# Attention steps taken from a written list of names instead of a rule over estimated times

## The chip, the cores and the metric

The kernel runs on one core of a Trainium2 chip. The metric is the device time in microseconds (us) of the whole launch. The kernel before took 1698.75 us, the median of 3 runs (1696.91 to 1700.2).

The engines are named as in the profile: PE is the matmul engine (PEld its weight loads), DVE the vector engine, ACT the scalar engine, POOL the GpSimd engine, SP the engine that issues most of the DMAs. Each works through its own instructions strictly in the order in which the program gives them, and waits at an instruction until what it needs has been finished elsewhere.

## The reference, cut to what matters

One inference step of a two-layer encoder, in float32, on 512 prompt rows and 64 sample rows (576 columns in the kernel, which works on transposed activations). Each layer:

```python
h = rmsnorm(x, w['g_mix_norm'])
proj = h @ w['w_in']                                   # one projection for three mixers
qa, ka, va, qg, kg, vg, ag, rg, cq, ckv, kr_raw = jnp.split(proj, offsets, axis=-1)
o_a = stick_breaking_attention(qa, [past, ka], [past, va])      # "sb", 4 heads of 64
o_b = gla_recurrence(qg, kg, vg, log_a, s0) , times silu(rg)    # "gla", blocks of 16 rows
o_c = mla_attention(cq, ckv, kr_raw, ...)                       # "mla", 8 heads, latent keys
x = x + jnp.concatenate([norm(o_a), norm(o_b), norm(o_c)], -1) @ w['w_out']
x = x + memory_cross_attention(rmsnorm(x, ...), mem_k, mem_v, w)  # mem_k, mem_v from mem_prompt
h = rmsnorm(x, w['g_ffn_norm'])
x = x + (jax.nn.silu(h @ w['w_gate']) * (h @ w['w_up'])) @ w['w_down']
```

Stick-breaking attention takes scores, a running sum along the keys (a scan in the kernel) and an exponential; the mla queries are projected from a low-rank `cq`, normalised per head and rotated.

## The kernel before, in words

Large matrix products are made from float32 split in a high and a low part (`wH`, `wL` of a weight, `hH`, `hL` of an activation), three matmuls for one. Weights arrive by DMA as `wraw`; ACT makes `wH` from it and DVE makes `wL`.

The attention stage of a layer (the part that the change touches) is cut into generators. Each `yield` ends one *step*: the instructions that are issued between two yields. Several generators are alive at once, and class `Order` (from line 750) takes one step of one of them at a time. Whatever it takes is issued at once, so the order of the steps is the order in which the instructions stand on PE and, within small limits of the scheduler behind it, on DVE, ACT and POOL too.

The generators that the change and the prediction speak of, with the names of the tiles in the trace (the digit is the layer) and the letters by which the new list calls their steps:

- `win()` (line 1028, letter W): the projection, some 39 steps, most of them 24 matmuls into `win0.D`. It has rank 10, that is, it is meant as filler. Its last steps make the columns `rg` (for the gate of gla) and `cq` (for the mla queries); a `cq` step (`nat`, line 925) also issues small statistics (`win0.s`, `win0.j`) on ACT, DVE and POOL. T10 to T14 turn a tile of `cq` (`win0.T<-ident,win0.j`, results to `win0.cT`).
- sb units (`sb_units`, line 1135; b0 to b7, two alive at a time), three steps each: scores (`sb0.S<-win0.sbk,win0.qo`), which also issue the chain of copies on ACT, scans on DVE and masks on POOL that make the weights `sb0.sg`; transposes (`sb0.T<-ident,sb0.sg`) with the copies to `sb0.PT`, one on ACT and one on DVE; and the product with the values (`sb0.T<-sb0.PT,win0.sbv`). c is the norm of their output.
- the turning of the memory rows (j, `wout0.T<-ident,wout0.mem`, results to `wout0.mH` and `wout0.mL`) and the projection of the memory keys and values (k0, 8 steps of 24 matmuls into `wout0.D`).
- mla query units (`mlaq_units`, line 1197; d0 to d9, three alive): scores of one row tile (`mlaq0.S<-mlaq0.wH,win0.cT`), followed by a chain that goes back and forth between ACT, DVE and POOL, and, in a second step, transposes (`mlaq0.T<-ident,mlaq0.j`). e are the units for keys and values (`mlak0`), f the attention itself, g the norms, h the sample rows.
- the output projection `wout` (line 1251): k1 is its part for gla (16 steps of six matmuls, `wout0.D<-gla0.mix,wout0.wH`), k2 for sb, k3 for mla. Each step ends in one DVE addition `X<-X,wout0.D`. Rank 10, so filler too.

What sets the order before is the rule in `Order.run` (line 791). Class `Clock` (line 39) keeps an estimate of when each tile is written and when each engine is free. Among the live generators the rule looks at those whose inputs, by that estimate, are there by the time PE is through with what it has (plus `SLACK`), and takes the lowest rank first:

```python
now = max(clock.pe + SLACK, min(at(x) for x in free))
x = min((x for x in free if at(x) <= now), key=lambda x: (x["rank"], at(x), x["n"]))
```

The same class orders the cross attention behind it in each layer; that and the feed-forward part are not touched. Nearly every instruction is recorded at one helper line, L195, so the rows below are told apart by their tiles.

Of the kernel before, what the change touches and what calls it, by code (L numbers as in the profile page):

```python
# [216 lines left out]
def tile_hybrid(ctx, tc, ins, outs):  # L217
    clock = tc.clock = Clock()
# [528 lines left out]
    class Order:  # L747
# [23 lines left out]
        def line(self, units, depth=2, rank=0, name=None, tag="S"):  # L771

            self.lines.append({"units": list(units), "depth": depth, "rank": rank, "live": 0, "name": name, "ph": phase[0],
                               "tag": tag})
# [1039 lines left out]
```

## Time and profile before

| quantity | value |
|---|---|
| median of 3 runs | 1698.75 us (1696.91 to 1700.2) |
| the profiled execution's own time | 1699.62 us |
| its span, first to last instruction | 1697.9 us |
| PE busy | 1648.0 us (97%), 12279 instructions |
| DVE busy | 1211.8 us (71%) |
| ACT busy | 898.4 us (53%) |
| POOL busy | 206.6 us (12%) |
| chain that ended last | PE 77%, DVE 12%, ACT 4%, issue 3% |

Span less PE busy is the time in which PE did nothing, about 50 us. The launch lies 1.7 us around the span. The attention stage of layer 0 runs from about 25 to 385 us, that of layer 1 some 835 us later; between them stand cross attention and the feed-forward part, where PE has next to no idle time.

### The profile page before, as it was taken

To read this page: it belongs to the slowest core of one execution; us is meant where nothing else is said; L and a number is where in the kernel's file an instruction comes from. 1 tells how busy PE (TensorE), PEld (TensorE's weight loads), DVE (VectorE), ACT (ScalarE), POOL (GpSimd) and SP (SyncE) were. 2 spreads that over 40 slices of the span, in tenths; PEclk is the share of its full clock that TensorE was granted. 3 is DMA by queue.
4 is the path that set the end of the run, shared out by engine and by line. 5 is a ranking of instruction groups with operands and counts; after the bars stand their busy time and mean duration, and the time that the engine had idled before them with its cause. 6 is when DMAs were issued, how large, how long until landed. Compare 5 with 4: busy or idle time off the path is not lost.

```text
span 1697.9 us, 30894 instructions
## 1 busy us (share of the span) xinstructions
PE 1648.0 (97%) x12279; PEld 1534.6 (90%) x12279; DVE 1211.8 (71%) x2462; ACT 898.4 (53%) x1915; POOL 206.6 (12%) x303
## 2 busy tenths in 40 slices
...
GB/s 166 114 49 82 44 128 35 26 58 82 61 57 94 100 81 95 97 81 98 79 79 91 78 51 88 94 26 26 85 65 51 86 92 97 87 88 100 85 91 56
DMA packets 113648, 133.31 MB, mean 79 GB/s; under 512 B 10610, under 2 KB 95712, under 8 KB 113504
## 3 DMA queue, kind: packets, MB, share of 16 engines
...
q0 software_dynamic: 352, 0.03, 0.0%
...
## 4 chain that ended last, share of the span: by engine, by line
PE 77%; DVE 12%; ACT 4%; issue 3%; POOL 2%; DMA 1%; POOLq 0%; ACTq 0%; DVEq 0%; SPq 0%
PE ffn0.D L195 9%; PE ffn1.D L195 9%; PE ffn0.T L195 7%; PE ffn0.S L195 7%; PE ffn1.T L195 7%; PE ffn1.S L195 6%; PE win1.D L195 5%; PE win0.D L195 4%; PE cross0.D L195 3%; PE wout1.D L195 2%; PE wout0.D L195 2%; PE cross1.D L195 2%; PE cross1.T L195 1%; PE cross0.T L195 1%; PE mlap0.T L195 1%
## 5 line engine op out<-in xcount | busy, mean ns | idle before, releaser
L195 ACT ACTIVATE ffn1.wH<-ffn1.wraw 128x1024 fp32r<-128x1024 f32 x64 | 59.3, 927 | 116.5 <-PE ffn1.T L195 61.5
L195 ACT ACTIVATE ffn0.wH<-ffn0.wraw 128x1024 fp32r<-128x1024 f32 x64 | 59.3, 927 | 111.9 <-PE ffn0.T L195 60.8
L195 DVE TENSOR_TENSOR ffn1.sL<-ffn1.sum,ffn1.sH 128x1024 fp32r<-128x1024 f32 x40 | 48.9, 1222 | 39.7 <-ACT ffn1.sH L195 39.6
L195 DVE TENSOR_TENSOR ffn0.sL<-ffn0.sum,ffn0.sH 128x1024 fp32r<-128x1024 f32 x40 | 48.9, 1222 | 39.7 <-ACT ffn0.sH L195 39.6
L195 DVE TENSOR_TENSOR ffn0.wL<-ffn0.wraw,ffn0.wH 128x1024 fp32r<-128x1024 f32 x64 | 67.5, 1055 | 8.2 <-ACT ffn0.wH L195 7.6
L195 DVE TENSOR_TENSOR ffn1.wL<-ffn1.wraw,ffn1.wH 128x1024 fp32r<-128x1024 f32 x64 | 67.5, 1055 | 8.2 <-ACT ffn1.wH L195 7.6
L195 POOL TENSOR_TENSOR ffn0.u<-ffn0.u,ffn0.u 128x576 f32<-128x576 f32 x6 | 10.0, 1672 | 459.8 <-DVE ffn0.wL L195 452.8
L195 PE MATMUL ffn1.D<-ffn1.bT,ffn1.sH 128*128 128x288 f32 x320 | 65.1, 295 | 0.2 <-ACT ffn1.part L195 0.2
L195 PE MATMUL ffn0.D<-ffn0.bT,ffn0.sH 128*128 128x288 f32 x320 | 65.2, 295 | 0.1
L195 ACT ACTIVATE ffn0.sH<-ffn0.sum 128x1024 fp32r<-128x1024 f32 x40 | 42.2, 1056 | 21.1 <-PE ffn0.S L195 20.9
L195 ACT ACTIVATE ffn1.sH<-ffn1.sum 128x1024 fp32r<-128x1024 f32 x40 | 42.2, 1055 | 21.1 <-PE ffn1.S L195 20.9
L195 PEld LDWEIGHTS ffn1.D<-ffn1.bT,ffn1.sH 128*128 128x128 f32 x320 | 51.6, 189 | 1.0 <-ACT ffn1.part L195 0.9
L195 PEld LDWEIGHTS ffn0.D<-ffn0.bT,ffn0.sH 128*128 128x128 f32 x320 | 51.6, 189 | 0.6 <-ACT ffn0.part L195 0.3
L195 PE MATMUL ffn1.D<-ffn1.bT,ffn1.sL 128*128 128x288 f32 x160 | 47.5, 297 | 0.0
L195 PE MATMUL ffn0.D<-ffn0.bT,ffn0.sL 128*128 128x288 f32 x160 | 47.5, 297 | 0.0
L195 PE MATMUL win1.D<-win1.wH,ffn0.hH 128*128 128x256 f32 (+1 forms) x160 | 47.2, 295 | 0.0
L195 PE MATMUL win0.D<-win0.wH,in.hH 128*128 128x256 f32 (+1 forms) x160 | 46.9, 293 | 0.0
L195 PE MATMUL win0.D<-win0.wL,in.hH 128*128 128x256 f32 (+1 forms) x160 | 45.9, 287 | 0.3 <-DVE win0.wL L195 0.3
L195 PE MATMUL win1.D<-win1.wL,ffn0.hH 128*128 128x256 f32 (+1 forms) x160 | 45.8, 286 | 0.4 <-DVE win1.wL L195 0.4
L195 PE MATMUL win1.D<-win1.wH,ffn0.hL 128*128 128x256 f32 (+1 forms) x160 | 45.7, 286 | 0.0
L195 PE MATMUL win0.D<-win0.wH,in.hL 128*128 128x256 f32 (+1 forms) x160 | 45.7, 286 | 0.0
L195 ACT ACTIVATE ffn1.part<-ffn1.D 128x288 f32<-128x288 f32 x60 | 24.5, 409 | 38.8 <-PE ffn1.D L195 38.8
...
## 6 DMA issues: line engine op xcount, KB each, us to landing
...
```

What stands on the lines that cost most here:

```text
L195: r = fn(*args, **kw)
```

## The change

The rule gives way to a list, `STEPS`, of 317 step names for one layer. A generator gets a letter (and a count for each new one of its kind), and `Order.run` takes the live generator that the list names next. Only the attention stage passes a list; layer 1 uses the same one without `G0` (the gains, which only layer 0 loads). The cross attention goes on by the rule. The steps themselves, and with them every instruction, are the same; helper line L195 becomes L209.

```diff
+STEPS = """
...
+W0*3 b0 j0 W0*2 b1 b0 j0 W0*3 b0 b2 W0 b1 j0 W0 b1 W0 b3 b2 j0 T10 W0 b2 b4 b3 T11 T12 b3 b5 W0 b4 W0 b4 b6 T13 k0 b5
+k0 b5 b7 Y0 p0 b6 k0 T14 b6 Y1 p1 b7 k0 b7 Y2 c0*2 d0 d1 k0 c1 Y3 k0 d2 c1 k0 d0 d3 d1 d4 d2 d5 k0*2 k1 d3 d6 k1 d4 d7
...
+"""
@@ class Order
-        def add(self, gen, rank=0, ready=0.0, line=None, done=None, tag="T"):
+            self.count, self.taken = {}, []
+
+        def add(self, gen, rank=0, ready=0.0, line=None, done=None, tag="T", name="x"):
             self.n += 1
+            k = self.count[name] = self.count.get(name, -1) + 1
...
-        def run(self):
+        def run(self, steps=None):
+
+            steps = [w.split("*")[0] for w in (steps or "").split() for _ in range(int((w + "*1").split("*")[1]))]
             self.start()
             while self.tasks:
-                at = lambda x: max(x["ready"], clock.room(x["tag"]))
                 free = [x for x in self.tasks if x["after"] is None or x["after"] in self.events]
-                now = max(clock.pe + SLACK, min(at(x) for x in free))
-                x = min((x for x in free if at(x) <= now), key=lambda x: (x["rank"], at(x), x["n"]))
+                if steps:
+                    x = next(x for x in free if x["name"] == steps[len(self.taken)])
+                else:
+                    at = lambda x: max(x["ready"], clock.room(x["tag"]))
+                    now = max(clock.pe + SLACK, min(at(x) for x in free))
+                    x = min((x for x in free if at(x) <= now), key=lambda x: (x["rank"], at(x), x["n"]))
+                self.taken.append(x["name"])
...
-        od.run()
+        od.run(STEPS.replace("G0", "") if l else STEPS)
```

Written in the same letters, the rule's own order in the stretch of the sb units was `W0*3 b0 j0 W0 b1 b0 j0 W0*2 b0 b2 b1 j0 W0*2 b1 b3 b2 j0 T10 W0 b2 b4 b3 T11 W0*2 b3 b5 b4 T12 W0*2 b4 b6 T13 b5 k0 T14 k0 b5 b7 p0 b6 Y0 k0 b6 Y1 p1 b7 k0 b7 Y2 k0 c0*2 d0 d1 c1`, and then `Y3 k0 d2 c1 k0 d0 d3 d1 d4 d2 d5 k0*2 k1 d3 d6 d4 d7 d5 d8 k1*3 d6 d9 e0 k1 d7 k1*2 d8 k1 d9 e1 e2`. From `d3 d6` on the new list has, behind one k1, `d4 d7 k1*2 d5 d8 k1*2 d6 d9 e0 k1 d7 k1*2 d8 k1 e1 e2 k1*2 d9`. Ahead of that stretch and behind it the two lists differ by small shifts: in the gla part one W stands a place earlier and T8 some later, and among the sample rows near the end `h1` comes before `h0`.

Three places on PE, rows in PE's order with the tile numbers of the program.

The first is in layer 0 around the transposes of the second sb unit (b1, `sb0.T<-ident,sb0.sg`); `win0.D` is a projection step, `sb0.S` the scores of b2, `wout0.T` the turning of memory rows. Before:

```order
L195 MATMUL win0.D_1736<-in.hH_136,win0.wL_1554 128x288
L195 MATMUL sb0.T_1686<-sb0.PT_1685,win0.sbv_279 64x128 x4
L195 MATMUL sb0.S_1771<-win0.sbk_278,win0.qo_276 128x384
L195 MATMUL sb0.S_1783<-win0.sbk_278,win0.qo_276 128x384
L195 MATMUL sb0.T_1796<-ident,sb0.sg_1661 128x128 x4
L195 MATMUL sb0.T_1802<-ident,sb0.sg_1675 128x128 x4
L195 MATMUL wout0.T_1808<-ident,wout0.mem_1490 128x128 x4
L195 MATMUL win0.D_1832<-win0.wH_1824,in.hH_135 128x256
L195 MATMUL win0.D_1832<-win0.wL_1825,in.hH_135 128x256
```

Now:

```order
L209 MATMUL win0.D_1806<-win0.wH_1802,in.hH_136 128x256
L209 MATMUL win0.D_1806<-win0.wL_1803,in.hH_136 128x256
L209 MATMUL win0.D_1806<-win0.wH_1802,in.hL_138 128x256
L209 MATMUL sb0.T_1839<-ident,sb0.sg_1661 128x128 x4
L209 MATMUL sb0.T_1845<-ident,sb0.sg_1675 128x128 x4
L209 MATMUL wout0.T_1851<-ident,wout0.mem_1463 128x128 x4
L209 MATMUL win0.D_1864<-win0.wH_1798,in.hH_135 128x256
L209 MATMUL win0.D_1864<-win0.wL_1799,in.hH_135 128x256
```

A whole projection step of 24 matmuls now stands between the scores of b2 (which lie just ahead of these rows) and the transposes of b1, where nothing stood; the next one still follows `wout0.T`.

The second is the product of the fourth sb unit with its values (b3, `sb0.T<-sb0.PT,win0.sbv`, six matmuls). Before, it came behind two projection steps; `sb0.S` are the scores of b5, `win0.T` is T12:

```order
L195 MATMUL sb0.T_1980<-sb0.PT_1979,win0.sbv_279 64x128 x6
L195 MATMUL sb0.S_2068<-win0.sbk_278,win0.qo_277 128x512
L195 MATMUL sb0.S_2080<-win0.sbk_278,win0.qo_277 128x512
L195 MATMUL sb0.T_2093<-ident,sb0.sg_1958 128x128 x4
L195 MATMUL sb0.T_2099<-ident,sb0.sg_1970 128x128 x4
L195 MATMUL win0.T_2105<-ident,win0.j_2022 128x128 x2
L195 MATMUL win0.D_2112<-win0.wH_1824,in.hH_135 64x256
```

Now `sb0.T_1963` is the product of b2, `sb0.T_2044<-ident` the transposes of b3 and `sb0.T_2044<-sb0.PT` its product:

```order
L209 MATMUL sb0.T_1963<-sb0.PT_1962,win0.sbv_279 64x128 x6
L209 MATMUL sb0.S_2019<-win0.sbk_278,win0.qo_276 128x512
L209 MATMUL sb0.S_2031<-win0.sbk_278,win0.qo_276 128x512
L209 MATMUL sb0.T_2044<-ident,sb0.sg_1941 128x128 x3
L209 MATMUL sb0.T_2049<-ident,sb0.sg_1953 128x128 x3
L209 MATMUL win0.T_2054<-ident,win0.j_1889 128x128 x2
L209 MATMUL sb0.S_2075<-win0.sbk_278,win0.qo_277 128x512
L209 MATMUL sb0.T_2044<-sb0.PT_2043,win0.sbv_279 64x128
L209 MATMUL sb0.S_2087<-win0.sbk_278,win0.qo_277 128x512
L209 MATMUL win0.T_2061<-ident,win0.j_1931 128x128 x2
L209 MATMUL sb0.T_2044<-sb0.PT_2043,win0.sbv_279 64x128 x5
L209 MATMUL win0.D_2099<-win0.wH_1798,in.hH_135 64x256
```

Between the transposes of b3 and its product now stand T11, the scores of b5 and T12, and no projection step.

The third is among the mla queries, behind the scores of d8 (before, `mlaq0.S_2915`) and of d7 (now, the first two rows); `mlaq0.T_2909` and `mlaq0.T_2933` are the transposes of d5, `wout0.D<-gla0.mix` the steps of k1. Before:

```order
L195 MATMUL mlaq0.S_2915<-mlaq0.wH_2761,win0.cT_1821 128x384
L195 MATMUL mlaq0.S_2915<-mlaq0.wL_2762,win0.cT_1821 128x384
L195 MATMUL mlaq0.S_2915<-mlaq0.wH_2761,win0.cT_1821 128x384 x2
L195 MATMUL mlaq0.S_2915<-mlaq0.wL_2762,win0.cT_1821 128x384
L195 MATMUL mlaq0.S_2915<-mlaq0.wH_2761,win0.cT_1821 128x384
L195 MATMUL wout0.D_2944<-gla0.mix_2317,wout0.wH_2823 128x288
L195 MATMUL mlaq0.T_2909<-ident,mlaq0.j_2773 96x128 x4
L195 MATMUL wout0.D_2944<-gla0.mix_2317,wout0.wH_2823 128x288
L195 MATMUL wout0.D_2944<-gla0.mix_2317,wout0.wL_2824 128x288
L195 MATMUL wout0.D_2944<-gla0.mix_2317,wout0.wH_2823 128x288 x2
```

Now:

```order
L209 MATMUL mlaq0.S_2888<-mlaq0.wH_2761,win0.cT_1795 128x384
L209 MATMUL wout0.D_2917<-gla0.mix_2314,wout0.wH_2823 128x288 x2
L209 MATMUL wout0.D_2917<-gla0.mix_2314,wout0.wL_2824 128x288
L209 MATMUL wout0.D_2917<-gla0.mix_2314,wout0.wH_2823 128x288 x2
L209 MATMUL wout0.D_2917<-gla0.mix_2314,wout0.wL_2824 128x288
L209 MATMUL wout0.D_2925<-gla0.mix_2314,wout0.wH_2823 128x288 x2
L209 MATMUL wout0.D_2925<-gla0.mix_2314,wout0.wL_2824 128x288
L209 MATMUL wout0.D_2925<-gla0.mix_2314,wout0.wH_2823 128x288 x2
L209 MATMUL wout0.D_2925<-gla0.mix_2314,wout0.wL_2824 128x288
L209 MATMUL mlaq0.T_2933<-ident,mlaq0.j_2773 96x128 x4
```

Two steps of k1 now stand ahead of the transposes of d5, and another (not among the rows) ahead of those of d4; before, the transposes of d5 came after one matmul of the first of these.

## Rows read from the trace of the kernel before

**Rows 1.** The page, its first part: span, then busy time by engine.
```profile
span 1697.9 us, 30894 instructions
...
PE 1648.0 (97%) x12279; PEld 1534.6 (90%) x12279; DVE 1211.8 (71%) x2462; ACT 898.4 (53%) x1915; POOL 206.6 (12%) x303
```

**Rows 2.** Waits of PE, 25 to 400 us: us in total, times, longest.
```profile
PE mlaq0.T L195 <- POOL mlaq0.j L195: 3.6, 6, 1.4
PE sb0.T L195 <- DVE sb0.PT L195: 2.6, 2, 1.8
PE gla0.S L195 <- POOL gla0.vm L195: 2.4, 1, 2.4
PE win0.T L195 <- DVE sb0.PT L195: 1.4, 1, 1.4
PE wout0.T L195 <- DVE wout0.mL L195: 1.0, 1, 1.0
PE wout0.T L195 <- ACT win0.qo L195: 1.0, 1, 1.0
```

**Rows 3.** Waits of PE, 860 to 1230 us (layer 1).
```profile
PE mlaq1.T L195 <- POOL mlaq1.j L195: 3.7, 6, 1.5
```

**Rows 4.** Windows: length, busy PE PEld DVE ACT POOL, granted clock, DMA.
```profile
140.00:175.00 35.00, 30.75 (x231) 25.51 (x230) 26.37 (x50) 18.36 (x53) 13.58 (x21) 0.95 0.20 63
175.00:210.00 35.00, 31.56 (x280) 27.15 (x279) 27.10 (x49) 23.37 (x59) 13.29 (x23) 1.00 0.15 50
210.00:225.00 15.00, 14.72 (x119) 13.72 (x117) 9.99 (x30) 10.94 (x24) 1.62 (x3) 1.00 0.41 130
225.00:250.00 25.00, 21.94 (x155) 19.98 (x156) 23.55 (x89) 18.80 (x45) 13.37 (x25) 1.00 0.35 118
250.00:275.00 25.00, 23.93 (x172) 21.24 (x171) 23.31 (x88) 21.16 (x74) 6.63 (x16) 1.00 0.13 44
275.00:350.00 75.00, 74.72 (x506) 53.89 (x504) 59.73 (x192) 54.17 (x161) 2.09 (x6) 1.00 0.09 29
350.00:385.00 35.00, 33.37 (x294) 29.77 (x290) 26.63 (x51) 22.64 (x56) 10.05 (x6) 1.00 0.28 91
...
166.15:169.55 3.40, 3.40 (x20) 2.00 (x15) 1.47 (x5) 2.45 (x10) 0.55 (x1) 0.50 0.02 5
```

**Rows 5.** Timeline of PE, 163 to 176.6 us: start, duration, instruction, idle before.
```profile
165.73 1.60 PE L195 MATMUL sb0.T<-sb0.PT,win0.sbv 128*64 128x128 f32 x14 [1.85 <-DVE sb0.PT L195]
...
170.03 0.36 PE L195 MATMUL win0.D<-win0.wH,in.hH 128*128 128x256 f32 x1
...
172.86 0.28 PE L195 MATMUL win0.D<-win0.wH,in.hL 128*128 128x256 f32 x1
...
176.41 0.41 PE L195 MATMUL win0.T<-ident,win0.j 128*128 128x128 f32 x2 [0.60 <-DVE win0.j L195]
```

**Rows 6.** The chain that ended last, 156 to 170 us, two of its pieces.
```profile
163.14 1.02 DVE sb0.kp L195
...
165.08 0.61 DVE sb0.PT L195
```

**Rows 7.** Timeline of ACT and of DVE, 175 to 183 us.
```profile
177.03 0.52 ACT L195 ACTIVATE sb0.PT<-sb0.T 128x384 f32<-128x384 f32 x1
...
179.43 0.53 DVE L195 COPY sb0.PT<-sb0.T 128x384 f32<-128x384 f32 x1
...
182.98 0.35 DVE L195 TENSOR_SCALAR win0.j<-win0.j,win0.s 128x256 f32<-128x256 f32 x1 [0.67 <-POOL win0.s L195]
```

**Rows 8.** Timeline of PE, 228 to 247.2 us.
```profile
232.58 0.64 PE L195 MATMUL mlaq0.T<-ident,mlaq0.j 128*96 128x128 f32 x4 [1.45 <-POOL mlaq0.j L195]
...
244.32 0.38 PE L195 MATMUL wout0.D<-gla0.mix,wout0.wH 128*128 128x288 f32 x1
...
246.53 0.29 PE L195 MATMUL wout0.D<-gla0.mix,wout0.wL 128*128 128x288 f32 x1
```

**Rows 9.** Groups of DVE instructions, 225 to 275 us: count | busy, mean ns | idle before.
```profile
L195 DVE TENSOR_TENSOR X<-X,wout0.D 128x288 f32<-128x288 f32 x18 | 7.8, 444 | 0.6 <-PE wout0.D L195 0.6
```

More of the change, by code (lines that the diff above doesn't have):

```diff
@@ L36 @@
 FFN_GROUPS = [(0, 1), (1, 2), (3, 2), (5, 2), (7, 2), (9, 2)]
+STEPS = """
+W0*3 G0 W0*4 T0 W0 T1 W0 T2 W0 T3 a0 W0 T4 a0 W0 a0 W0*3 S0*2 l0 W0 l0 S0 l0*2 l1 W0 l1*3 l2 S0 W0 l2 W0 l2*2 l3 S0 W0
+Z0*2 l3*3 l4 S0 Z0 W0 l4*3 Z0 W0 m0 Z0 T5 T6 W0 Z0 m0 W0 n0 n1 T7 T9 n0 n2 n1 n3 n2 n4 n3 n4 T8 o0 W0 o1 o0 o1 i0 j0
+W0*3 b0 j0 W0*2 b1 b0 j0 W0*3 b0 b2 W0 b1 j0 W0 b1 W0 b3 b2 j0 T10 W0 b2 b4 b3 T11 T12 b3 b5 W0 b4 W0 b4 b6 T13 k0 b5
+k0 b5 b7 Y0 p0 b6 k0 T14 b6 Y1 p1 b7 k0 b7 Y2 c0*2 d0 d1 k0 c1 Y3 k0 d2 c1 k0 d0 d3 d1 d4 d2 d5 k0*2 k1 d3 d6 k1 d4 d7
+k1*2 d5 d8 k1*2 d6 d9 e0 k1 d7 k1*2 d8 k1 e1 e2 k1*2 d9 e1 e3 k1 e2 e4 k1*2 f0 e3 f1 e4 k1*2 k2 f0 f1 e5 k2 f0 f2 f1
+f3 k2 e6 e7 f2 f3 e6 e7 f2 f4 f3 f5 e8 k2 e9 f4 f5 k2 e8 f4 f6 f5 e9 f7 f6 f7 f6 k2 f8 f7 e10 k2 e10 f9 f8*2 f10 f9
+k2*3 f10 f9 f11 f10 f12 g0*2 f11 k2 f12 f11 f13 g1 f12 g1 k2 g2 f13 k2 g2 f13 g3 k2*2 g3 k2*2 h1 h0 k3 h2 h1*2 k3*2
+h0*2 h3 h1 h2 h0*2 h2 k3 h2 h1 h3 h2 h3 k3 h3*2 k3*13
+"""
 class Clock:
@@ L754, in __init__ @@
             self.tasks, self.lines, self.events, self.n = [], [], {}, 0
-        def add(self, gen, rank=0, ready=0.0, line=None, done=None, tag="T"):
+            self.count, self.taken = {}, []
+        def add(self, gen, rank=0, ready=0.0, line=None, done=None, tag="T", name="x"):
             self.n += 1
+            k = self.count[name] = self.count.get(name, -1) + 1
             self.tasks.append({"rank": rank, "ready": ready, "n": self.n, "gen": gen, "line": line, "done": done,
-                               "ph": phase[0], "tag": tag, "after": None})
+                               "ph": phase[0], "tag": tag, "after": None, "name": f"{name}{k}"})
         def later(self, fn, tag="T"):
@@ L765, in once @@
                 yield
-            self.add(once(), 0, clock.last, tag=tag)
+            self.add(once(), 0, clock.last, tag=tag, name="T" if phase[0][:3] == "win" else "Y")
         def event(self, name):
@@ L773, in line @@
             self.lines.append({"units": list(units), "depth": depth, "rank": rank, "live": 0, "name": name, "ph": phase[0],
[L774 removed]
+                               "tag": tag, "letter": "abcdefghijklmnopqr"[len(self.lines)]})
         def start(self):
@@ L781, in start @@
                     phase[0] = ln["ph"]
-                    self.add(gen, ln["rank"], max((self.events[x] for x in need), default=0.0), ln, done, ln["tag"])
+                    self.add(gen, ln["rank"], max((self.events[x] for x in need), default=0.0), ln, done, ln["tag"],
+                             ln["letter"])
         def end(self, task):
@@ L1046, in win @@
             od.event("vg")
-            od.add(lat_past())
+            od.add(lat_past(), name="S")
             w = load_w(wi[:, 0:256], KD, 256)
```

6 lines of the change are left out of this document (3 added, 3 removed).

## The prediction

> **What bounds the kernel now.** The page first: PE is busy 1648.0 us of a span of 1697.9 us [rows 1]. The change issues the same instructions, so it can only touch the other 50 us, or shift work so that PE waits anew. The waits of PE by stretch come next. In layer 0 they name few causes: the mla queries on POOL, the sb units on the DVE copy `PT`, the gla states once on POOL, and three single ones among the sb units [rows 2]. Layer 1 has the same list, with 3.7 where layer 0 has 3.6 [rows 3], so one layer is worked out and doubled.
>
> The windows show where this lies [rows 4]. Among the sb units, 140 to 210 us, PE is idle 35.00 - 30.75 = 4.25 and 35.00 - 31.56 = 3.44 us, together 7.7. From 210 to 275 us, the mla queries, it is 0.28 + 3.06 + 1.07 = 4.4. From 275 to 350 us PE is full (0.28 idle), and the end, 350 to 385, has 1.6. The reader is to see two unlike places: among the sb units no engine is full (DVE 26.37 of 35.00), so each step waits for the latency of a chain, and filler on PE hides it. Among the mla queries DVE is busy 23.55 of 25.00 us: there a wait of PE may be DVE's pace, which no filler shortens.
>
> The clock adds to the first place. After the longest wait, 1.85 us ahead of the value product of b1 [rows 5], PE ran 3.40 us at a granted clock of 0.50 [rows 4], the 1.2 GHz level. At half speed that is 3.40 / 2 = 1.7 us lost.
>
> **The sb units.** Idle 7.7 plus 1.7 by the clock is 9.4 us in a layer to be won at most. Filler is a projection step, 24 matmuls from 170.03 to 172.86 us [rows 5], some 3 us. It was spread unevenly: b1's product has one such step ahead of it and still waits 1.85 us.
>
> The chain of waits says why. DVE does the scans of b2, whose scores were issued ahead of b1's transposes, first (1.02 us each, the last at 163.14), and only then, at 165.08, copies b1's `PT` for 0.61 us [rows 6]. PE comes too early by what DVE must do for b2. The list puts one projection step ahead of b1's transposes and one behind `wout0.T`; an earlier one goes ahead of b1's scores. So the waits of 1.0 on `wout0.mL` and 1.0 on `win0.qo` [rows 2], each shorter than a 3 us step that is now ahead of it, go altogether. At b1's product PE arrives about 3 us later against b2's chain, less the 2.4 us or so of waits that it no longer has ahead; the chain itself loses some of what it waited for. I leave 0 to 1 us of the 1.85 and take 0.5. The rest of `PT`'s 2.6 us (2.6 - 1.85 = 0.75, at b4) goes, since a memory step k0 is issued around it, and so does T14's 1.4, since T14 now comes a unit later.
>
> What hid the waits behind, the list takes from elsewhere. The product of b3 had two projection steps ahead of it and waited for nothing; now T11, the scores of b5 and T12 follow b3's transposes directly, and that costs. ACT copied its half of b3's `PT` from 177.03 to 177.55, DVE its half from 179.43 to 179.96, behind b4's scans [rows 7]. In those coordinates PE would be through with T11 by about 176.6 (it starts it at 176.41 [rows 5], two matmuls). With half of b5's scores it is at some 177.0 and waits about 0.55 for ACT. The other half brings it to about 178.2, and T12 reuses what DVE's copy reads: 179.96 - 178.2 = 1.8 us of wait. Behind it stand the rest of b3's product and a projection step, which nobody needs soon. The 0.60 ahead of T11 [rows 5] stays. Left over: 0.60 + 0.55 + 1.8 + 0.5 = 3.45, and the gain is 9.4 - 3.45 = 5.95 if the clock does not fall, 4.25 if the new 1.8 us brings the same 1.7 back. Waits of 1.45 in the mla window left the clock at 1.00 [rows 4, 8], one of 1.85 did not; the new one lies nearer the second but is an estimate, so I take the middle, 5.1.
>
> On this the Trainium skill (TensorE: Matmul & The Clock Gate, Part 1) says that the half clock is the default and that activity releases it, and its examples of a relapse are waits a good deal longer than any here. By that rule the new wait would cost no clock, and the term would be 5.95. The trace does not agree in so far as a wait of 1.85 us was followed by the lower level; the sum keeps the middle.
>
> **The mla queries.** The scores of d0 and d1 are now issued ahead of a memory step k0 instead of behind it, 3 us sooner, in a window in which DVE has room (9.99 of 15.00 us [rows 4]). The first wait of this stretch, 1.45 ahead of d2's transposes [rows 8], should go with that. Then one step of k1 is put ahead of d4's transposes and two ahead of d5's. Such a step is six matmuls; the 17 of three steps from 244.32 to 246.53 [rows 8] start 2.21 / 16 = 0.14 us apart, so it is 0.8 us of PE. But each brings an addition into `X` of 0.444 us [rows 9] onto DVE, where the next unit's chain stands behind it. DVE's idle time is 1.45 us in 225 to 250 and 1.69 in 250 to 275 [rows 4], so up to 3.1 us of waiting can be turned into work at best. Bounds: 0, if DVE sets the pace throughout, and 3.9, if all but 0.5 of the 4.4 goes. I take 2.0: the first wait whole and a third of the rest.
>
> **Everything else.** Two additions of k1 fewer remain for the stretch from 275 us, which is full (74.72 of 75.00 [rows 4]), so nothing is late there. At the end h1 goes ahead of h0 while ACT and DVE are busy with both; 0 to 1 us lost, 0.5 taken, from the 1.6 us idle there now. The wait of 2.4 on `gla0.vm` [rows 2] stays: POOL's work for it and the steps ahead of it are where they were. DMA queues: weights are loaded by the same steps and shift by one step, 3 us, within the same order on SP, and none of the waits in [rows 2, 3] is on a DMA; I cost them at nothing, and at up to 1 us a layer if a `wraw` comes late.
>
> **Sum.** 5.1 + 2.0 - 0.5 = 6.6 us a layer, 13.2 for both. The profiled execution took 1699.62 us, so 1686.4; the median of the three runs lies 0.9 below it, hence 1685.5 us.
>
> **Rivals.**
> - *DVE keeps its pace.* The mla stretch gains nothing, the clock falls once at T12: 4.25 - 0.5 = 3.75 a layer, 7.5 in all, 1691 us. For it: 23.55 of 25.00 us on DVE. Against it: the first wait lies where DVE had idle time before.
> - *Nearly all waits go.* Left are T11's 0.60 among the sb units and 0.5 among the queries: 8.8 + 3.9 = 12.7 a layer, 25.4 in all, 1673 us. Against it stand the missing filler at b3.
> - *The order is only another one.* The chains (scan, mask, copy) give the pace, PE's waits come back in other places at the same size: 1699 us.
> - *Slower: DVE held up at its head.* Each `cq` step puts two small statistics on DVE, and the second waits for POOL, 0.67 us of an idle DVE [rows 7]. Four such steps now stand a place sooner, ahead of the scans of b3 and b4. If scans and `PT` come later by that, up to 4 x 0.67 = 2.7 us, the waits at b1 and b3 are 1.85 and 0.55 + 1.8 + 2.7, each with a fall of the clock (2 x 1.7), and T11's 0.60: 10.9 against the 9.4 of now. With nothing won among the queries and 0.5 lost at the end that is 2.0 a layer, 1703 us. It decides from the point at which `PT` of b3 is ready 4 us or more after PE gets there. Against it: PE too comes later by each of these steps, some 3 us.
>
> **How the numbers follow.** Chances: the forecast 0.50 (its own range 1681 to 1691, from 4.25 to 7 among the sb units and 0.5 to 3.5 among the queries), DVE's pace 0.19, nearly all 0.06, only another order 0.10, slower 0.15. A measurement of this kernel tells 0.2%, 3.4 us, from no change. Faster by more is the first three, 0.75; within it the fourth, 0.10; slower 0.15. The range leaves out the slower case (0.15) and the lower half of the case in which nearly all goes (0.03): 1676 to 1700.
>
> **What would show it.** Right: among the sb units of layer 0, PE's idle time about 3.5 us (from 7.7) with no wait on `wout0.mL`, `win0.qo` or at T14; new waits of T12 on `sb0.PT` near 1.8 us and of b3's product on ACT near 0.5; the wait at d2 gone; idle time from 210 to 275 us about 2.4; the same in layer 1. Wrong: a wait at T12 over 4 us, more than one stretch of granted clock 0.50 among the sb units, POOL's `mlaq0.j` still over 3 us in PE's waits, or new waits on a DMA. Outside the attention stage nothing may change; if it does, the sum rests on the wrong stage.

## The result, and the profile after

| | before | after |
|---|---|---|
| median | 1699.42 us (1696.91 to 1700.2, 4 runs) | 1680.39 us (1678.53 to 1681.31, 4 runs) |
| profiled span | 1697.9 us | 1679.5 us |
| PE busy | 1648.0 us | 1644.6 us |
| span less PE busy | 49.9 us | 34.9 us |

The ratio is 0.989, 95% interval 0.987 to 0.991: 19.0 us faster, where 13.2 were forecast (1685.5 us). Executions of one kernel differ with the mean clock granted to PE: of nine of the kernel before, the two at 0.995 of full speed took 1695.59 and 1696.07 us, the seven at 0.991 to 0.993 took 1698.96 to 1700.60; over 87 executions of thirteen of the kernels here the slope inside a kernel is 1.2 us for each thousandth. The first part of the page after, against [rows 1]:

```profile
span 1679.5 us, 30904 instructions
PE 1644.6 (98%) x12279; PEld 1537.0 (92%) x12279; DVE 1208.1 (72%) x2462; ACT 898.3 (53%) x1915; POOL 213.1 (13%) x303
```

The two profiled spans are 18.4 us apart. The same 12279 matmuls leave PE 15.0 us less idle. The other 3.4 us are in PE's busy time, at which the sum had looked for the clock only. The waits of PE after, from 25 to 400 us (us in total, times, longest), against [rows 2], and the row of layer 1 against [rows 3]:

```profile
PE gla0.S L209 <- POOL gla0.vm L209: 2.4, 1, 2.4
PE wout0.D L209 <- DVE X L209: 2.3, 2, 2.1
PE win0.T L209 <- DVE sb0.PT L209: 0.9, 1, 0.9
...
PE mlaq0.T L209 <- POOL mlaq0.j L209: 0.7, 1, 0.7
PE sb0.T L209 <- DVE sb0.PT L209: 0.5, 2, 0.3
...
PE mlaq1.T L209 <- POOL mlaq1.j L209: 0.7, 1, 0.7
```

The waits on `mlaq0.j` fell from 3.6 to 0.7, those of `sb0.T` from 2.6 to 0.5; the ones on `wout0.mL` and `win0.qo` are gone. New is 2.1 on `X`. The windows after, columns as in [rows 4]:

```profile
140.00:175.00 35.00, 34.58 (x279) 31.08 (x277) 27.30 (x54) 21.13 (x58) 14.85 (x23) 1.00 0.21 67
175.00:210.00 35.00, 33.41 (x272) 27.13 (x268) 27.21 (x48) 23.91 (x58) 12.26 (x21) 0.90 0.26 84
210.00:225.00 15.00, 15.00 (x112) 14.51 (x111) 13.81 (x44) 12.74 (x29) 5.87 (x8) 1.00 0.30 89
225.00:250.00 25.00, 24.06 (x165) 21.94 (x163) 23.45 (x83) 19.17 (x44) 13.79 (x24) 1.00 0.31 100
250.00:275.00 25.00, 24.62 (x172) 21.26 (x171) 22.54 (x90) 21.91 (x84) 4.28 (x11) 1.00 0.22 79
275.00:350.00 75.00, 74.30 (x561) 54.96 (x560) 61.54 (x198) 54.81 (x170) 1.90 (x6) 1.00 0.05 16
350.00:385.00 35.00, 32.63 (x254) 31.41 (x253) 24.15 (x36) 21.38 (x38) 10.49 (x6) 1.00 0.26 91
...
179.98:186.81 6.83, 6.37 (x32) 5.71 (x33) 5.35 (x10) 2.56 (x6) 0.58 (x3) 0.50 0.01 2
```

PE's idle time among the sb units is 0.42 + 1.59 = 2.0 us (7.7 before), among the mla queries 0.00 + 0.94 + 0.38 = 1.3 (4.4), at the end 2.4 (1.6). From 275 to 350 us it is idle 0.7 us (0.3 before), but has done 561 matmuls where it did 506. The windows lie at the same times and so hold somewhat other work; the stretch has therefore to be cut at the same two instructions. From the first scores of the mla attention (`mlap0.S`) to the last of the sample rows (`mlas0.S`), the window of before and of after:

```profile
266.03:355.98 89.95, 89.67 (x646) 66.80 (x644) 72.34 (x236) 65.02 (x203) 3.41 (x10) 1.00 0.07 25
```
```profile
261.42:346.32 84.90, 84.42 (x627) 63.99 (x625) 71.43 (x234) 63.61 (x201) 3.51 (x10) 1.00 0.08 26
```

PE is full in both, and the stretch is 5.05 us shorter. Of that, 17 matmuls of the output projection `wout0.D` (162 and 145 in the stretch) are done elsewhere, 12 of k1 ahead of it, in the time won among the queries, and 5 of k3 behind it: 17 x 0.14 = 2.4 us. The other 2.7 us are the same work done more densely. Layer 1 shows the same stretch at 89.94 and 84.91 us. The groups of PE in these two windows (count | busy, mean ns of one), before and after:

```profile
L195 PE MATMUL wout0.D<-sb0.mix,wout0.wH 128*128 128x288 f32 x64 | 16.6, 328 | 0.0
L195 PE MATMUL mlap0.T<-mlap0.PT,mlak0.v 128*64 128x128 f32 x160 | 13.5, 282 | 0.0
```
```profile
L209 PE MATMUL wout0.D<-sb0.mix,wout0.wH 128*128 128x288 f32 x64 | 15.2, 319 | 0.0
L209 PE MATMUL mlap0.T<-mlap0.PT,mlak0.v 128*64 128x128 f32 x160 | 11.7, 279 | 0.0
```

The 160 value products (`mlap0.T<-mlap0.PT`, 64 columns of weights each) take 13.5 us of PE before and 11.7 after, though one record lasts the same (282 and 279 ns): they overlap more. (The trace has two records for one of these products, so 160 records are 80 products: the product of b3, one and then five matmuls in the program's order, is x2 and x10 in the trace.)

### The profile page after: what moved, and what is told of

Its sections match the earlier page's. It is cut to its first block, busy times and chain, and to the rows that moved or that the text cites. A ratio compares the mean times of both kernels' runs of the same rounds, so it can differ in the third digit from the quotient of the medians.

```text
span 1679.5 us, 30904 instructions
## 1 busy us (share of the span) xinstructions
PE 1644.6 (98%) x12279; PEld 1537.0 (92%) x12279; DVE 1208.1 (72%) x2462; ACT 898.3 (53%) x1915; POOL 213.1 (13%) x303
## 3 DMA queue, kind: packets, MB, share of 16 engines
q8 instruction: 97, 1.59, 0.4%
## 4 chain that ended last, share of the span: by engine, by line
PE 78%; DVE 10%; issue 4%; ACT 3%; POOL 2%; DMA 2%; POOLq 0%; ACTq 0%; DVEq 0%
PE ffn0.D L209 9%; PE ffn1.D L209 9%; PE ffn0.T L209 7%; PE ffn1.T L209 7%; PE ffn0.S L209 7%; PE ffn1.S L209 6%; PE win1.D L209 5%; PE win0.D L209 3%; PE wout1.D L209 2%; PE wout0.D L209 2%; PE cross1.D L209 2%; PE cross0.D L209 2%; PE cross0.T L209 1%; PE cross1.T L209 1%; PE mlap0.T L209 1%
## 5 line engine op out<-in xcount | busy, mean ns | idle before, releaser
L209 ACT ACTIVATE ffn1.wH<-ffn1.wraw 128x1024 fp32r<-128x1024 f32 x64 | 59.3, 927 | 116.5 <-PE ffn1.T L209 61.1
L209 ACT ACTIVATE ffn0.wH<-ffn0.wraw 128x1024 fp32r<-128x1024 f32 x64 | 59.3, 927 | 111.8 <-PE ffn0.T L209 60.7
L209 DVE TENSOR_TENSOR ffn0.sL<-ffn0.sum,ffn0.sH 128x1024 fp32r<-128x1024 f32 x40 | 48.8, 1221 | 39.7 <-ACT ffn0.sH L209 39.7
L209 DVE TENSOR_TENSOR ffn1.sL<-ffn1.sum,ffn1.sH 128x1024 fp32r<-128x1024 f32 x40 | 48.9, 1221 | 39.7 <-ACT ffn1.sH L209 39.6
L209 DVE TENSOR_TENSOR ffn0.wL<-ffn0.wraw,ffn0.wH 128x1024 fp32r<-128x1024 f32 x64 | 67.5, 1055 | 8.3 <-ACT ffn0.wH L209 7.6
L209 DVE TENSOR_TENSOR ffn1.wL<-ffn1.wraw,ffn1.wH 128x1024 fp32r<-128x1024 f32 x64 | 67.5, 1055 | 8.3 <-ACT ffn1.wH L209 7.6
L209 POOL TENSOR_TENSOR ffn0.u<-ffn0.u,ffn0.u 128x576 f32<-128x576 f32 x6 | 10.0, 1673 | 460.6 <-DVE ffn0.wL L209 453.6
L209 PE MATMUL ffn1.D<-ffn1.bT,ffn1.sH 128*128 128x288 f32 x320 | 65.3, 295 | 0.1
L209 PE MATMUL ffn0.D<-ffn0.bT,ffn0.sH 128*128 128x288 f32 x320 | 65.1, 295 | 0.2
L209 ACT ACTIVATE ffn0.sH<-ffn0.sum 128x1024 fp32r<-128x1024 f32 x40 | 42.2, 1055 | 21.1 <-PE ffn0.S L209 20.9
L209 ACT ACTIVATE ffn1.sH<-ffn1.sum 128x1024 fp32r<-128x1024 f32 x40 | 42.2, 1055 | 21.1 <-PE ffn1.S L209 20.9
L209 PEld LDWEIGHTS ffn0.D<-ffn0.bT,ffn0.sH 128*128 128x128 f32 x320 | 51.6, 189 | 0.9 <-ACT ffn0.part L209 0.9
L209 PEld LDWEIGHTS ffn1.D<-ffn1.bT,ffn1.sH 128*128 128x128 f32 x320 | 51.6, 189 | 0.8 <-ACT ffn1.part L209 0.4
L209 PE MATMUL win0.D<-win0.wH,in.hH 128*128 128x256 f32 (+1 forms) x160 | 47.8, 299 | 0.0
L209 PE MATMUL ffn0.D<-ffn0.bT,ffn0.sL 128*128 128x288 f32 x160 | 47.5, 297 | 0.0
L209 PE MATMUL ffn1.D<-ffn1.bT,ffn1.sL 128*128 128x288 f32 x160 | 47.5, 297 | 0.0
L209 PE MATMUL win0.D<-win0.wL,in.hH 128*128 128x256 f32 (+1 forms) x160 | 46.8, 292 | 0.3 <-DVE win0.wL L209 0.3
L209 PE MATMUL win1.D<-win1.wH,ffn0.hH 128*128 128x256 f32 (+1 forms) x160 | 46.7, 292 | 0.0
L209 PE MATMUL win0.D<-win0.wH,in.hL 128*128 128x256 f32 (+1 forms) x160 | 46.6, 291 | 0.0
L209 PE MATMUL win1.D<-win1.wL,ffn0.hH 128*128 128x256 f32 (+1 forms) x160 | 45.5, 285 | 0.4 <-DVE win1.wL L209 0.4
L209 PE MATMUL win1.D<-win1.wH,ffn0.hL 128*128 128x256 f32 (+1 forms) x160 | 45.4, 284 | 0.0
L209 ACT ACTIVATE ffn1.part<-ffn1.D 128x288 f32<-128x288 f32 x60 | 24.5, 409 | 38.8 <-PE ffn1.D L209 38.8
```

What stands on the lines that cost most here:

```text
L209: r = fn(*args, **kw)
```

## The experiments

Letters and names are those of the list. "Rule" is the order of before, written in these letters. All were timed beside the kernel before. Two counts of PE's order, one layer, from the first `mlap0.S` to the end of the mla attention, come up again: how often the output tile or the kind of input *changes* from one matmul to the next, and in how many *pieces* the value products lie. Before: 103 changes, 17 pieces; after: 90 and 11. Differences from the kernel after compare medians of different sessions; the ratio to the kernel before, timed beside each, is given with them.

**Undoing one part at a time.**

```diff
- i0 j0 W0*3 b0 j0 W0*2 b1 b0 j0 W0*3 b0 b2 W0 b1 j0 W0 b1 W0 b3 b2 j0 T10 W0 b2 b4 b3 T11 T12 b3 b5 ... k0 b7 Y2
+ W0 i0 j0 W0*3 b0 j0 W0 b1 b0 j0 W0*2 b0 b2 b1 j0 W0*2 b1 b3 b2 j0 T10 W0 b2 b4 b3 T11 W0*2 b3 b5 b4 T12 ... k0 b7 Y2
```

> The list everywhere but in the stretch of the sb units (from the first b0 to Y2), where the steps stand in the rule's order, in both layers. Theory 1, the forecast's: that stretch is worth 5.1 us a layer, so 1680.4 + 10.2 = 1690.6 us. Theory 2, from PE's time per matmul in the two traces, which counts delays that no idle time shows: 6.1 us in layer 0 and 8.1 in layer 1, so 1694.6. Rival, only another order: 1680 to 1682. In the trace the waits on wout0.mL, win0.qo, sb0.PT 1.85 and T14 1.4 come back, and those at T12 (0.9) and b3 (0.2) go.

1688.15 us (1686.61 to 1692.97, 6 runs), ratio 0.994 [0.992, 0.995]: 7.8 us lost, below both sums (10.2 and 14.2). PE's busy time from 140 to 175 us is back at 30.39, from 175 to 210 at 32.09, and so are the waits:

```profile
PE sb0.T L209 <- DVE sb0.PT L209: 2.6, 2, 1.9
...
PE win0.T L209 <- DVE sb0.PT L209: 1.4, 1, 1.4
PE wout0.T L209 <- DVE wout0.mL L209: 1.0, 1, 1.0
PE wout0.T L209 <- ACT win0.qo L209: 1.0, 1, 1.0
```

The idle time among the sb units belongs to their order.

```diff
- c0*2 d0 d1 k0 c1 Y3 ... k1 d3 d6 k1 d4 d7 k1*2 d5 d8 k1*2 d6 d9 e0 k1 d7 k1*2 d8 k1 e1 e2 k1*2 d9 e1 e3 k1 e2 e4
+ k0 c0*2 d0 d1 c1 Y3 ... k1 d3 d6 d4 d7 d5 d8 k1*3 d6 d9 e0 k1 d7 k1*2 d8 k1 d9 e1 e2 k1*2 e1 e3 k1 e2 e4 k1*2
```

> The list everywhere but among the mla queries (from Y2 to the last e4 before f0), where the steps stand in the rule's order, in both layers. Theory 1, the forecast's: 2.0 us a layer, so 1684.4 us. Theory 2, DVE keeps its pace and the order there is worth nothing: 1680 to 1681. By PE's time per matmul in the two traces 1.7 and 1.0 us: 1683.1. The waits of PE on mlaq0.j should be 3 us or more a layer again (now 0.7).

1693.47 us (1691.77 to 1696.35, 6 runs), ratio 0.9965 [0.995, 0.998]: the largest loss of a single part, 13 us, where 4.0 at most were expected. The waits on `mlaq0.j` are back at 3.6 us in a layer, and by the first `mlap0.S` PE has been idle 3.1 us longer than in the kernel after (it is only 1.5 us later, since the kernel after had run longer at the lower clock by then). The next 3.7 us are lost behind it, in the stretch of the mla attention, whose steps were left as the list has them, with the same 145 matmuls of `wout0.D` as after and the same idle time:

```profile
262.92:351.51 88.59, 88.11 (x626) 64.73 (x625) 70.23 (x225) 63.63 (x196) 3.29 (x10) 1.00 0.07 25
```

PE's order there has 115 changes and 19 pieces: the scheduler behind the list interleaves neighbouring steps on PE too, and what stands ahead alters how it cuts them. So the order of the steps alone doesn't fix PE's order.

```diff
- k1*2 f0 e3 f1 e4 k1*2 k2 f0 f1 e5 k2 f0 f2 f1 f3 k2 e6 e7 f2 f3 e6 e7 f2 f4 f3 f5 e8 k2 e9 ... g2 f13
+ f0 e3 f1 e4 k1*4 k2 f0 f1 e5 k2 f0 f2 f1 f3 e6 e7 f2 f3 k2 e6 f2 f4 f3 f5 e7 e8 e9 f4 f5 ... g2 f13 k2
```

> The list everywhere but in the mla attention (from f0 to the last g2 and f13), where the steps stand in the rule's order of layer 0, in both layers. Theory 1, the forecast's: PE is full there in either order, nothing: 1680.4 us. Theory 2: although PE shows no idle time, the list starts its matmuls closer, 1.5 us a layer by PE's time per matmul: 1683.4.

1689.35 us (1685.78 to 1692.16, 6 runs), ratio 0.994 [0.993, 0.995]: 9.0 us lost, where 0 or 3.0 were expected. No more idle time in the stretch (0.08 us), and yet 89.02 us long; nine more matmuls of `wout0.D` in it are 9 x 0.14 = 1.3 of the 4.1 that it is longer. So PE loses time there without waiting. 105 changes, 18 pieces.

```diff
- h1 h0 k3 h2 h1*2 k3*2 h0*2 h3 h1 h2 h0*2 h2 k3 h2 h1 h3 h2 h3 k3 h3*2
+ h0 h1 h0 k3 h2 h0 h1 h0 k3 h3 h1 h0 h2 k3 h1 h2 h1 h3 h2*2 k3 h3 k3 h3*2
```

> The list everywhere but from g3 to the end of the attention stage (sample rows h, output projection k3), where the steps stand in the rule's order of layer 0, in both layers. Theory 1: the new wait of 2.1 us for X near the end, with the half clock behind it in layer 1, comes from this part of the list; with the rule's order the wait is 0.9 again and the time 1680.4 - 2 x 1.2 - 1.7 = 1676.3 us. Theory 2: that wait comes from the order in which DVE gets the weights of the cross attention, which the estimating clock sets anew whatever the order here, so it stays: 1680 to 1681.

1679.08 us (1676.59 to 1681.78, 4 runs), ratio 0.988 [0.9865, 0.989], not told apart from the kernel after; the waits on `X` fall from 2.3 to 1.1 us, so the long one does come from this part of the list. What lies behind the 2.1 is seen in the kernel after, timelines of DVE, POOL and PE:

```profile
363.79 2.46 DVE L209 TENSOR_TENSOR cross0.wL<-cross0.wraw,cross0.wH 128x1024 fp32r<-128x1024 f32 x1
366.17 1.95 DVE L209 SCALAR_TENSOR_TENSOR wout0.hL<-X,gT,wout0.hH 128x576 fp32r<-128x576 f32 x1
368.04 0.81 DVE L209 TENSOR_TENSOR X<-X,wout0.D 128x288 f32<-128x288 f32 x2
368.77 1.21 DVE L209 TENSOR_TENSOR cross0.wL<-cross0.wraw,cross0.wH 128x1024 fp32r<-128x1024 f32 x1
...
361.41 6.10 POOL L209 TENSOR_TENSOR wout0.u<-wout0.u,wout0.u 128x576 f32<-128x576 f32 x3
...
368.54 0.40 PE L209 MATMUL wout0.D<-mlas0.mixH,wout0.wH 128*128 128x288 f32 x1 [2.14 <-DVE X L209]
```

While POOL squares `wout0.u`, DVE's subtraction `cross0.wL` takes 2.46 us; the next one, behind POOL's end, 1.21. The addition into `X` queues behind both stretched instructions. That POOL stretches them is read from the overlap and was not tested; beside other multiplications of POOL in this trace the same subtraction took 1.2 to 1.3 us, so an overlap alone does not decide it.

> The rule's order (of layer 0, in both layers) everywhere but among the sb units, which follow the list. If the parts add up, and the sb units are worth what undoing them cost (7.8 us, 1688.15 against 1680.39), 1700.4 - 7.8 = 1692.6 us. If undoing one part costs more than the part alone brings, because the parts lend each other filler, nearer 1696. By the forecast's 5.1 us a layer 1690.2.

The reverse of the first: the list in the sb stretch (from `i0 j0` to `Y2`), the rule elsewhere. 1685.1 us (1680.39 to 1687.04, 5 runs), ratio 0.993 [0.991, 0.994]. That is 12.4 us, 6.2 a layer, for the sb units alone. Part of it is clock: these runs had a mean granted clock of 0.9950 and those of the kernel before beside them 0.9929, some 2.5 us. What is left, about 10 us or 5 a layer, is near the forecast's 5.1. Undoing one part each, e1, e2 and e3, cost 8, 13 and 9 us, together more than the 19 of the whole: they don't stand by themselves, as the cut of the mla attention already showed.

**The new waits of the list.**

```diff
- b3 T11 T12 b3 b5 W0 b4 W0
+ b3 T11 W0 b3 T12 b5 b4 W0
```

> The list with one change: the projection step W that stood behind the scores of b5 now stands ahead of the product of b3 (b4 b3 T11 W0 b3 T12 b5 b4 W0 b4 b6 in place of b4 b3 T11 T12 b3 b5 W0 b4 W0 b4 b6). Theory 1: the three waits of 0.2, 0.2 and 0.9 at b5, b3 and T12 go, with the half clock behind them (1.7 us a layer in the profiled run): 1680.4 - 2 x 1.3 = 1677.8, and 1674.4 if the clock goes with them. Rival: b4's transposes now follow b5's scores directly and wait for the masks on POOL instead, so the same time.

1679.42 us (1678.94 to 1681.63, 4 runs), ratio 0.989 [0.988, 0.991]. T12's wait goes, others come, in the next unit and at the memory rows:

```profile
PE sb0.T L209 <- DVE sb0.PT L209: 1.1, 2, 0.8
...
PE wout0.T L209 <- DVE wout0.mL L209: 0.7, 1, 0.7
...
PE sb0.S L209 <- ACT sb0.sg L209: 0.6, 1, 0.6
```

The time is the rival's, though the new waits are not those on POOL's masks that it named. Filler is short there; a step put at one place is missing at another.

```diff
- S0 Z0 W0 l4*3 Z0
+ S0 Z0 l4*2 W0 l4 Z0
```

> The list with one change: the projection step W that stood ahead of the second step of the last gla state unit (l4) stands ahead of its last step, the one that waits 2.4 us for gla0.vm from POOL. Theory 1: a step of 24 matmuls hides that wait and the half clock behind it goes: 1680.4 - 2 x 2.4 = 1675.6, with the clock 1672.2. Rival: the two steps before it now come without filler and wait for their own copies, 1 us or so each, and the time stays within 2 us.

1679.73 us (1679.34 to 1680.84, 4 runs), ratio 0.989 [0.988, 0.991]. The wait on `gla0.vm` fell from 2.4 to 2.0 only, and the two steps ahead did not come to wait 1 us each: only the rival's time came out. POOL and DVE in the kernel after, then POOL in this run:

```profile
91.82 6.32 POOL L209 TENSOR_TENSOR gla0.vm<-win0.vg,blk 64x256 f32<-64x256 f32 x2 [1.76 <-PE gla0.S L209]
...
92.85 4.89 DVE L209 TENSOR_TENSOR_SCAN gla0.U<-win0.vg,gla0.U 128x264 f32<-128x264 f32 x8
```
```profile
89.22 6.32 POOL L209 TENSOR_TENSOR gla0.vm<-win0.vg,blk 64x256 f32<-64x256 f32 x2 [1.76 <-PE gla0.S L209]
```

POOL's two multiplications start once PE's scores before them are done, and take 6.32 us in either kernel: 0.82 for the first, 5.53 for the second, which lies beside eight scans of DVE and ends with them. In that time PE does the same projection step of 24 matmuls in both, so the edit put no more filler ahead of the wait than was there.

**Changes and pieces in the mla attention.** The first try held PE strictly to the order of the steps, in the whole attention stage:

```diff
+        nc.chain.update(pe=None)
         od.run(STEPS.replace("G0", "") if l else STEPS)
+        nc.chain.clear()
```

> The list, and in the attention stage PE's instructions are held to the order in which the steps issue them (an order-only dependency between successive ones), so that no step is cut into pieces. In the stretch from the first to the last instruction of the mla attention PE then changes 62 times from one kind of work to another in place of 90, and no pair of value products (two heads in the two halves of the columns) is split (now 4 pieces of 11 are of odd length). Theory 1: much of what the list won in the mla attention, where PE shows no idle time, is fewer such changes, each costing 0.15 to 0.2 us; then that stretch gets 4 us shorter in each layer, less what strict order adds in waits: 1672 to 1677 us. Theory 2, changes cost nothing and the stretch is bound by DVE's pace: no shorter there, and strict order adds waits: 1681 to 1690.

1765.06 us (1761.27 to 1766.86, 4 runs), ratio 1.039 [1.037, 1.040]. PE has fewer changes (62) and waits everywhere, as for 4.1 us on `mlas0.pr` and 3.9 at T12. It shows that strict order costs some 85 us (part of it clock, 0.974 to 0.978 against 0.991 to 0.994), and nothing on the price of a change, which drowns in it.

The clean test exchanges two neighbouring steps, no filler among them:

```diff
- f0 e3 f1 e4 k1*2
+ f0 e3 e4 f1 k1*2
```

> The list with two neighbouring steps exchanged (e4 before f1, behind f0 e3), no filler moved. The scheduler behind the list cuts the steps in another way: in PE's order of the mla attention the kind of matmul now changes 117 times in a layer (90 with the list as it is), and the value products of the attention lie in 20 pieces (11). Theory 'changes of kind': each costs about 0.15 us with no idle time shown (3.7 us for 25 more in the run with the mla part on the rule): 27 x 0.15 x 2 = 8.1 us, 1688 us, ratio to before near 0.994, no more idle time of PE than the new kernel has (35 us). Rival 'pace and waits': one exchange moves no work that another engine waits for, time within 2 us of the new kernel, ratio 0.988 to 0.990; or a loss that is seen as idle time of PE.

1688.65 us (1688.03 to 1692.15, 5 runs), ratio 0.995 [0.993, 0.996]: 8.3 us slower than the kernel after, where 8.1 were expected. (The number of changes in this order is 117, the pieces are 20.) The same stretch, window and then groups:

```profile
258.02:347.20 89.18, 88.65 (x626) 64.43 (x625) 71.47 (x234) 64.57 (x201) 3.72 (x10) 1.00 0.08 25
```
```profile
L209 PE MATMUL wout0.D<-sb0.mix,wout0.wH 128*128 128x288 f32 x64 | 17.4, 339 | 0.0
L209 PE MATMUL mlap0.T<-mlap0.PT,mlak0.v 128*64 128x128 f32 x160 | 14.6, 284 | 0.0
```

The same matmuls, the same 0.5 us of idle time, 89.18 us for 84.90; layer 1 has 89.17 for 84.91. The value products take 14.6 us instead of 11.7. The timelines of PE show how. After (start, duration), and then this run:

```profile
270.28 1.09 PE L209 MATMUL mlap0.T<-mlap0.PT,mlak0.v 128*64 128x128 f32 x16
271.30 0.54 PE L209 MATMUL wout0.D<-sb0.mix,wout0.wH 128*128 128x288 f32 x2
...
288.22 1.09 PE L209 MATMUL mlap0.T<-mlap0.PT,mlak0.v 128*64 128x128 f32 x14
289.24 0.64 PE L209 MATMUL mlak0.T<-ident,mlak0.j 128*96 128x128 f32 x4
289.81 0.43 PE L209 MATMUL mlap0.T<-mlap0.PT,mlak0.v 128*64 128x128 f32 x2
290.17 0.53 PE L209 MATMUL wout0.D<-sb0.mix,wout0.wH 128*128 128x288 f32 x2
```
```profile
266.97 0.66 PE L209 MATMUL mlap0.T<-mlap0.PT,mlak0.v 128*64 128x128 f32 x8
267.56 0.70 PE L209 MATMUL mlap0.S<-mlak0.kT,win0.qT 96*128 96x256 f32 x2
...
292.76 0.65 PE L209 MATMUL mlap0.T<-mlap0.PT,mlak0.v 128*64 128x128 f32 x6
293.34 0.55 PE L209 MATMUL mlap0.T<-ident,mlap0.pr 128*128 128x128 f32 x3
```

Taken from the start of a piece to the start of what follows, 16 records last 1.02 us and 14 also 1.02, eight 0.59 and six 0.58, two 0.36. So a piece with an odd number of products (14, six and two records are seven, three and one product) takes as long as one with a product more. In the trace the products of a pair start within 0.01 us of each other, and the one left over in an odd piece runs by itself. The durations give about 0.22 us for each pair, a pair of which only one product is there included, and 0.145 for each piece.

This order has 20 pieces for 11 and 14 odd ones for four, that is, nine pieces and five pairs more: 9 x 0.145 + 5 x 0.22 = 2.4 us a layer. Summed from start to start, the value products do take 2.3 us longer. The 96 matmuls of k2 (`wout0.D<-sb0.mix`) take 17.8 us for 15.5, another 2.3; the other kinds give 0.4 back, and that is the 4.28. The k2 matmuls lie in 28 pieces for 19; one right behind another starts 0.13 us after it, the first of a piece holds PE for mostly 0.22 and at times 0.4 to 0.6. What those longest ones are spent on is open.

```diff
- f4 f5 k2 e8 f4 f6 f5
+ f4 f5 k2 f4 e8 f6 f5
```

> The control: the list with two other neighbouring steps exchanged (f4 before e8), which leaves PE's order with the same 90 changes and 11 pieces. Both theories: as the new kernel, ratio 0.988 to 0.990. If it is slower by 3 us or more, an exchange costs by itself and the theory of the changes has no footing.

1682.89 us (1679.85 to 1684.87, 5 runs), ratio 0.990 [0.9885, 0.992]. The interval overlaps that of the kernel after, and the stretch is the same to 0.01 us (in layer 1 too, 84.90 and 84.91):

```profile
262.39:347.28 84.89, 84.40 (x626) 63.99 (x625) 71.39 (x234) 63.60 (x201) 3.53 (x10) 1.00 0.08 26
```

So an exchange that leaves PE's pieces as they were costs nothing there.

```diff
- f5 e9 f7 f6 f7 f6 k2
+ f5 e9 f6 f7*2 f6 k2
```

> A third exchange (f6 before f7, behind e9): 102 changes of kind in a layer, 15 pieces. Theory 'changes of kind': 12 x 0.15 x 2 = 3.6 us, 1684 us, ratio near 0.991, between the two others. Rival 'pace and waits': ratio 0.988 to 0.990, or more idle time of PE.

1689.33 us (1686.78 to 1691.28, 5 runs), ratio 0.994 [0.993, 0.996].

```profile
261.76:350.57 88.81, 88.33 (x631) 65.86 (x630) 71.87 (x235) 64.18 (x201) 3.53 (x10) 1.00 0.08 25
```

The loss is there, without idle time, but 3.91 us a layer (0.7 of it five more matmuls of `wout0.D`) where 1.8 were expected. A flat price for a change is therefore wrong: 4.28 / 27 = 0.16 us in the one, (3.91 - 0.7) / 12 = 0.27 in the other, and that the expected loss of the first exchange came out to 0.2 us was luck. By pieces and pairs the value products should lose 4 x 0.145 + 4 x 0.22 = 1.5 us here (15 pieces, 12 odd); they lose 1.3, and k2 2.4. The same sum gives 1.5 for the kernel before (17 pieces, 10 odd), where they take 1.45 us longer, and 2.3 for the run with the query part on the rule (19 and 14), where it is 2.2. The prices were read with the results on the table, but from single pieces, not from the totals that they meet.

```diff
- b3 T11 T12 b3 b5 W0 b4 W0   ...   S0 Z0 W0 l4*3 Z0    ...   h1 h0 k3 h2 h1*2 k3*2 ...
+ b3 T11 W0 b3 T12 b5 b4 W0   ...   S0 Z0 l4*2 W0 l4 Z0  ...   h0 h1 h0 k3 h2 h0 h1 ...
```

> The three small mends together: the rule's order in the tail of each layer, one projection step between T11 and b3, one inside l4. Each alone came out 0.7 to 1.3 us below the new kernel, inside its spread. If they add: 1677.4 us, ratio near 0.987. If what stays is the pace of the chains: ratio 0.988 to 0.990.

1677.92 us (1674.47 to 1679.98, 4 runs), ratio 0.988 [0.986, 0.989]. The best median of all, near the 1677.4 of the case in which they add, but its interval overlaps that of the kernel after, and its four runs had a mean granted clock of 0.9942 against 0.9918: some 2.9 us, more than the 2.5 won. So no gain of the three mends is shown. The profiled run had one stretch at the lower clock, behind the start, instead of six.

## Why the prediction was right, and where its sum was off

**The sb units: right in kind, T12 mis-sized.** Forecast 5.1 us a layer: idle time from 7.7 to 3.45, and half a fall of the clock. Measured: 7.7 to 2.0, 5.7 won. The waits on `wout0.mL`, on `win0.qo`, at b1 and T14 went as said, and b3's product waits for ACT and T12 for DVE's `PT`, as said. PE, then DVE, around T12, against [rows 5, 7]:

```profile
174.37 1.13 PE L209 MATMUL sb0.S<-win0.sbk,win0.qo 64*128 64x512 f32 x4
...
176.73 1.12 PE L209 MATMUL sb0.S<-win0.sbk,win0.qo 64*128 64x512 f32 x2 [0.21 <-ACT sb0.sg L209]
178.09 0.43 PE L209 MATMUL sb0.T<-sb0.PT,win0.sbv 128*64 128x128 f32 x2 [0.24 <-ACT sb0.PT L209]
...
180.44 0.69 PE L209 MATMUL win0.T<-ident,win0.j 128*128 128x128 f32 x2 [0.86 <-DVE sb0.PT L209]
...
179.86 0.53 DVE L209 COPY sb0.PT<-sb0.T 128x384 f32<-128x384 f32 x1
```

T12 waits 0.86 us instead of 1.8, and T11's 0.60, which was to stay, is gone. DVE copies at 179.86 (179.43 in the forecast's coordinates); PE is there at 180.44 - 0.86 = 179.58 and not at 178.2, since each half of b5's scores takes 1.12 us and not 0.4 and 0.65 as the forecast had it. In b4 (174.37) both halves lie next to each other and take 1.13 us together; b3's product, put between those of b5, makes each run alone. The forecast priced a half as part of a pair.

**The clock: the pessimistic side.** The sum took half of 1.7 us. In this run the level fell at 179.98, beside a wait of 0.86, for 6.83 us: by the half speed that the forecast took, 3.4 lost where 1.7 were lost before, so layer 0 kept 5.7 - 1.7 = 4.0 of its gain. In layer 1 the stretch at 1002.4 became one at 1006.0, both 3.41 us, and the idle time won there (5.4) stayed whole. By the rule of the Trainium skill (TensorE: Matmul & The Clock Gate, Part 1) on idle gaps, which speaks of gaps a good deal longer, the 0.86 should have cost nothing; the trace does not agree. The same part also has a kernel that idles briefly and often and whose level goes up and down, which the prediction passed over. Nor does the length of a wait decide it: the run with only the sb part on the list waits 0.9 at T12 and 2.4 on `gla0.vm` like the others, and has no stretch at the lower level between 20.5 and 1679 us.

**The mla queries: right, low by a third.** Forecast idle 4.4 to 2.4, measured to 1.3; 3.1 won where 2.0 were taken (bounds 0 and 3.9; "the first wait whole and a third of the rest" is 1.45 + 2.95 / 3 = 2.4 by the forecast's own numbers). The wait at d2 went. DVE, which was held to be the pace by the first rival, is as busy as before (23.45 of 25.00 from 225 us) and PE does 24.06 instead of 21.94: the rival is refuted. Part of the time won appears as the 12 matmuls of k1 done ahead of the mla attention.

**"Everything else": the failed step.** The sum said that the stretch from 275 us "is full (74.72 of 75.00), so nothing is late there", and costed it at nothing. Nothing waits there, that was right; but the same matmuls can take 84.9 or 89.2 us without a wait. The term that was 0 measured 2.7 us a layer, 5.4 in both, nearly the whole of the missing 19.0 - 13.2 = 5.8. Of the 2.7 in layer 0, from start to start, the value products make 1.45 and the k2 matmuls 2.0, and the other kinds take 0.7 back. The lists differ in the mla attention too, as the diff of the third experiment shows, and PE's orders, from which the forecast took its three places, hold the 17 and the 11 pieces as well; it looked for waits where filler moved, and not at how the small products were cut.

**The end** lost 0.8 (idle 1.6 to 2.4) where 0.5 was taken, but by another way than "ACT and DVE busy with both": by additions into `X` behind DVE instructions that ran long beside POOL's.

Check of the sum, layer 0: sb 4.0, queries 3.1, denser PE 2.7, end -0.8, together 9.0; at the last transposes of cross attention the kernel after is 9.0 us ahead (461.72 and 470.73 us). At the same instruction of layer 1 it is 18.3 us ahead, of which 14.9 are idle time of PE, and 1.7 of those go to the clock: 13.2, the forecast's sum to the digit. That is in part luck. Counted between the same instructions in both layers, the sb units gave 11.1 - 1.7 = 9.4 where 10.2 were taken, the queries 5.7 where 4.0 were, and what lies behind lost 2.1 where 1.0 was. What the sum lacked is the other 5.1, denser PE, nearly all in the mla attention (the 5.4 above, where the moved matmuls are taken off at 0.14 us each). So the time, 1680.4, lies in the stated range (1676 to 1700) but just under the forecast's own 1681 to 1691, which by the bounds given with it would be 1679 to 1690.

The slower rival did not come: DVE's head is held for the same 0.67 us by `win0.s`, but b3's `PT` was ready 0.86 us after PE got there, not 4.
